# RWKV steps on one core: VectorE adds the old state, and residuals and outputs share one product with it

## The chip, the core and the metric

One core of a Trainium2 chip runs the whole program once: two network blocks on 512 tokens of 1024 channels, in fp32. The metric is the time of the program on the device in microseconds. Times of the rows below come from one profiled execution, counted from the start of its span.

The engines that matter here: TensorE (PE in the rows; PEld is its weight load) multiplies out of SBUF into PSUM banks; VectorE (DVE), ScalarE (ACT) and GpSimd (POOL) work on tiles; SyncE (SP) issues DMAs. Each engine takes its instructions in a fixed order, and semaphores hold an instruction until what it reads or overwrites is ready.

## The reference, cut to what matters

Only the RWKV-7 layer of the second block is touched. For each of 16 heads a state of 64 x 64 is carried through 512 tokens:

```python
def step(state, inp):
    r_t, w_t, k_t, v_t, a_t, b_t = inp
    sa = jnp.einsum('bhij,bhj->bhi', state, a_t)
    state = (state * w_t[:, :, None, :] + sa[..., None] * b_t[:, :, None, :]
             + v_t[..., None] * k_t[:, :, None, :])
    y_t = jnp.einsum('bhij,bhj->bhi', state, r_t)
    return state, y_t
...
_, ys = lax.scan(step, state0, seq_inputs)
```

Around it stand projections, a group norm of the outputs, a bonus term and a gate.

## The kernel before

A scheduler orders each engine's instructions at build time from a simulated timeline; TensorE and the others then run in that order.

The recurrence is computed in blocks of 64 tokens. A chunk is 128 channels, two heads side by side, and its state is a tile `SB` of 128 x 128 whose two 64 x 64 diagonal blocks are the heads' states. A unit is four chunks and half of the tokens, four steps of 64 tokens. Units 0 and 1 are the two halves of the channels in the first 256 tokens, units 2 and 3 the same in the second.

Before a unit's steps, `rwkv_prep` makes the decayed tiles `kr` (the keys' side k and the receptance r), `BN`, `PC` (the decay over a step) and the masked products `G`; `rwkv_inverse1` solves the triangular systems by 31 steps of two operations, each reading the one before (lines L1619 and L1621), on VectorE for units 0, 1 and 3 and on GpSimd for unit 2; ScalarE then copies the result (L1623), and `rwkv_inverse2` finishes on TensorE. After a unit's steps `rwkv_post` normalises the outputs on VectorE and transposes them. The program order is inverse 0, preparation, inverse 1, steps 0, half of the second tokens' preparation, steps 1, inverse 2, post 0, the other half, steps 2, inverse 3, post 1, steps 3, post 2, post 3.

`rwkv_steps` is the part that the change rewrites. `S0` is the old state, `S2` the new. For each of the four steps it goes four times over the four chunks:

- residuals: k against `S0`, plus `G` against the step's values; ScalarE copies them into `R` (L1688)
- corrections: `G` against `R`; ScalarE copies them into `UV` beside the values (L1692)
- new state: the identity against `S0`, plus `BN` against `UV`, added up in PSUM; ScalarE scales by `PC` into `S2` (L1703)
- outputs: r against `S0`, plus `G` against `UV` over all 128 rows; after every second step VectorE copies 128 x 128 outputs of two steps (L1710)

All products are recorded on one line, the helper's L1665. Two PSUM banks hold the four chunks, two chunks each, and the helper keeps the products of one bank in program order. A product in a bank waits for the read of the bank that stands before it in program order.

Of the kernel before, what the change touches and what calls it, by code (L numbers as in the profile page):

```python
# [105 lines left out]
def rwkv_consts():  # L106
    c = Cols()
    c.add("scan", np.tile((np.arange(256) % 64 != 0).astype(np.float32)[None, :], (128, 1)))
    s = np.arange(128)[:, None] % 64
    t = np.arange(64)[None, :]  # L110
    c.add("g", np.concatenate([(s < t), (s <= t)], 1).astype(np.float32))
    c.add("sel", (np.arange(80)[None, :] == 14 + np.arange(128)[:, None] // 64).astype(np.float32))
    return c.array()
# [83 lines left out]
class Core:  # L197
# [1122 lines left out]
    def rwkv(self, x, hn, xsrc):  # L1320

        nc = self.nc
        cst = self.t([128, 464], "cst2", 1)
        nc.gpsimd.dma_start(cst, self.I["cst2"])
        K = self.rk = {}
        K["scan"], K["gmask"] = cst[:, 0:256], cst[:, 256:384]
        sel = lambda m: cst[:, 398 - 2 * m:462 - 2 * m]
        for nm, src, a, b in (("w0h", "w0", 0.5, 0.0), ("a0h", "a0", 0.5, 0.0), ("nkk", "kk", -1.0, 0.0),
# [4 lines left out]
        o = self.voff["mu0"][0]  # L1333
# [5 lines left out]
        K["tmp"] = self.t([128, 256], "itmp", 1)  # L1339
        iv = K["iv"] = self.t([128, 256], "iv", 1)  # L1340

# [5 lines left out]
        K["SB"] = [[self.t([128, 128], "SB", 16) for _ in range(2)] for _ in range(8)]  # L1347
        for a, _ in K["SB"]:
            nc.gpsimd.memset(a, 0.0)

# [13 lines left out]
        def raw(name):  # L1364
# [3 lines left out]

        K["kr"] = [[self.rp.tile([128, 2, 256], F32, tag="rk", bufs=16, name="kr") for _ in range(8)]
                   for _ in range(2)]  # L1370

        def evac(m, i, ps):
            for h in range(2):
                nc.scalar.activation(K["kr"][h][m][:, i, :], ps[:, h * 256:h * 256 + 256], AF.Copy)


        mk, mr, mv = [], [], []
# [133 lines left out]
    def W2(self, name, u):  # L1511
# [6 lines left out]
        return hi, lo  # L1518

    def rwkv_prep(self, c, h, after):  # L1520

# [12 lines left out]
        kr = K["kr"][h][c]  # L1534
        k, r = kr[:, 0, :], kr[:, 1, :]
        r0, r1 = slice(0, 64), slice(64, 128)
# [18 lines left out]
        for g in range(2):  # L1555
            nc.sync.dma_start(nk[64 * g:64 * g + 64], K["ivd"][h, 2 * c + g:2 * c + g + 1].to_broadcast([64, 256]))
        nc.vector.scalar_tensor_tensor(nk, k, cc("nkk"), nk, op0=OP.mult, op1=OP.mult)
        bks = [BK[:, p::2, 1 - p, :] for p in range(2)]
# [4 lines left out]
        nc.vector.tensor_scalar(ta, ta, cc("ka1"), cc("ka2"), op0=OP.mult, op1=OP.add)  # L1563
        nc.vector.tensor_mul(ta, ta, k)
        nc.vector.tensor_mul(k, nk, tw)
        for p in range(2):
            nc.vector.tensor_mul(BK[:, p::2, p, :], ch(ta)[:, p::2], ch(L)[:, p::2])
        nc.vector.scalar_tensor_tensor(nk, r, self.v("rk", c), ta, op0=OP.mult, op1=OP.mult)
        nc.gpsimd.tensor_mul(r, r, Pm)
        return dict(c=c, kr=kr, BK=BK, bk=bk, BN=BN, G=G, PC=PC, rka=nk,  # L1570
                    M=gg.rearrange("q (u x c) -> q u x c", u=4, x=2))

    def rwkv_chunks(self, s):

        nc, K = self.nc, self.rk
        mm = nc.tensor.matmul
        BK, G, kr = s["BK"], s["G"], s["kr"]
        flat = lambda ap: ap.rearrange("p a b -> p (a b)")
        for g in range(2):
            rr = slice(64 * g, 64 * g + 64)  # L1580
            ps = self.bank("sc" if g else "tr")
            for n in range(4):
                mm(ps[:, n * 128:n * 128 + 128], flat(BK[rr, n]), kr[rr, :, n * 64:n * 64 + 64],
                   start=True, stop=True)
            p3, mk = ps.rearrange("p (n s) -> p n s", n=4), K["gmask"].unsqueeze(1).to_broadcast([128, 4, 128])
            nc.vector.tensor_mul(G[:, g], p3, mk)
        tp = self.bank("tr")
        for t in range(2):
            mm(tp[:, 2 * t:2 * t + 2], s["rka"][:, t * 128:t * 128 + 128], self.hsel, start=True, stop=True)
        bon = s["bon"] = self.t([128, 2, 2], "bon", 12)  # L1590
        nc.scalar.activation(bon, tp[:, 0:4].rearrange("p (t h) -> p t h", t=2), AF.Copy)
        for n in range(4):
            nc.tensor.transpose(tp[:, n * 128:n * 128 + 128], flat(BK[:, n]), self.ident)
        nc.scalar.activation(s["bk"], tp, AF.Copy)

    def rwkv_inverse1(self, u, e):
# [8 lines left out]
        for u0, m, o in us:  # L1605
            eng.dma_start(md[o].rearrange("u s t -> s u t"), m[u0:u0 + 64, :, 0:64])
        q0 = u % 2 * 64
# [21 lines left out]
        for b in (1, 0):  # L1629
            for u0, m, o in us:  # L1630
                eng.dma_start(m[u0 + 32 * b:u0 + 32 * b + 32, :, 32 * b:32 * b + 32],
                              md[o, rows(b), rows(b)].rearrange("u s t -> s u t"))
        return ins

    def rwkv_inverse2(self, u, sts):

        nc, K = self.nc, self.rk
        mm = nc.tensor.matmul
        ps = self.bank("av")
        Z = self.t([128, 512], "ea", 4, name="Z").rearrange("p (u s) -> p u s", u=16)  # L1640
        p4 = ps.rearrange("p (u s) -> p u s", u=16)
        G = K["ws"][u][1].rearrange("q (u x c) -> q u x c", u=16, x=2)
        hf = [(slice(64 * (1 - p), 64 * (1 - p) + 32), slice(64 * (1 - p) + 32, 64 * (1 - p) + 64)) for p in range(2)]
        for i in range(16):
            for p, (lo_, hi_) in enumerate(hf):
                mm(p4[hi_, i], G[lo_, i, p, 32:64], K["A11", u % 2][lo_, i], start=True, stop=True)
        for lo_, hi_ in hf:
            nc.scalar.activation(Z[hi_], p4[hi_], AF.Copy)
        for i in range(16):
            for p, (lo_, hi_) in enumerate(hf):  # L1650
                mm(p4[lo_, i], Z[hi_, i], G[hi_, i, p, 32:64], start=True, stop=True)
        for p, (lo_, hi_) in enumerate(hf):
            nc.vector.tensor_copy(G[lo_, :, p, 32:64], p4[lo_])

    def rwkv_steps(self, u, sts):
# [14 lines left out]
        for n in range(4):  # L1670
# [188 lines left out]
```

## Time and profile before

| | us |
|---|---|
| median of 3 runs | 3906.36 (3902.74 to 3907.86) |
| the profiled execution | 3908.79 |
| its span | 3907.0 |
| TensorE busy in the span | 3738.4 (96%) |
| VectorE busy | 1753.8 (45%) |
| ScalarE busy | 1507.1 (39%) |
| GpSimd busy | 1642.4 (42%) |

The span is what the rows count in; the execution's time holds some 2 us around it. The RWKV stage with its recurrence lies around 3030 to 3350 us of the span, where the granted clock of TensorE is lower than elsewhere (0.956 of full speed over the whole span).

### The profile page before, as it was taken

Reading aid. Unit: us, or ns where it says so; the run is one execution under the profiler, and the core shown is the slowest. Engines: PE = TensorE matmul, PEld = TensorE weight load, DVE = VectorE, ACT = ScalarE, POOL = GpSimd, SP = SyncE. Lnnn points to the kernel's source line nnn. Section 1 sums busy time; section 2 is a strip of 40 time slices with the busy share of each in tenths; the row PEclk is TensorE's granted clock in tenths of the full one; section 3 lists DMA queues with packets and bytes.
Section 4 is the critical chain, followed back from the end, with each engine's and each line's share of the span. In section 5 each row is a group of like instructions: output and inputs, shape, how many; then the busy total and the mean of one; then the engine's idle time right before and its main releaser. Section 6 shows DMA issues by size and latency. Waiting matters only on the chain.

```text
span 3907.0 us, 48377 instructions
## 1 busy us (share of the span) xinstructions
PE 3738.4 (96%) x18540; PEld 3000.4 (77%) x18540; DVE 1753.8 (45%) x3587; ACT 1507.1 (39%) x2677; POOL 1642.4 (42%) x900
## 2 busy tenths in 40 slices
PE   9999999999999999999998899999899899799998
PEld 8766777888896677778886777888676777688887
DVE  4553254533545424544436655222568545534123
ACT  4433333433344333334334634332454433343322
POOL 4422436444453233444444563444534321543444
PEclk9999999999999999999998999999999557899999
DMA  5311214233342122232221332222222311321222
GB/s 190 116 54 49 89 60 135 87 97 97 120 152 81 55 67 71 87 114 97 97 95 62 99 106 76 86 93 95 99 85 88 73 41 42 124 102 63 96 97 87
DMA packets 148952, 354.10 MB, mean 91 GB/s; under 512 B 50080, under 2 KB 60864, under 8 KB 148464
## 3 DMA queue, kind: packets, MB, share of 16 engines
q1 hardware_dynamic: 148448, 350.18, 27.6%
q8 instruction: 146, 2.39, 0.3%
q0 software_dynamic: 272, 0.82, 0.1%
q14 instruction: 86, 0.70, 0.1%
HBM read 332.56 MB, written 18.38 MB: 90 GB/s over the span
## 4 chain that ended last, share of the span: by engine, by line
PE 76%; DVE 9%; DMA 5%; POOL 4%; ACT 3%; issue 3%; SPq 0%; POOLq 0%; DVEq 0%; ACTq 0%
PE mm L322 13%; PE mm L323 13%; PE mm L324 13%; PE mm L384 5%; PE mm L383 5%; PE mm L385 5%; PE mm L1665 4%; POOL wlo L285 2%; PE av L383 2%; PE av L385 2%; PE av L384 2%; PE sc L823 2%; PE av L652 1%; PE tr L843 1%; ACT whi L284 1%
## 5 line engine op out<-in xcount | busy, mean ns | idle before, releaser
L285 POOL TENSOR_TENSOR wlo<-wst,whi 128x1024 fp32r<-128x1024 f32 (+2 forms) x524 | 1260.2, 2408 | 1784.2 <-PE mm L324 900.9
L284 ACT ACTIVATE whi<-wst 128x1024 fp32r<-128x1024 f32 (+2 forms) x524 | 548.7, 1048 | 1100.0 <-DMA wst<-in_wu 153.1
L322 PE MATMUL mm<-xTh,whi 128*128 128x512 f32 (+1 forms) x2208 | 833.1, 379 | 13.1 <-ACT whi L284 10.1
L323 PE MATMUL mm<-xTl,whi 128*128 128x512 f32 (+1 forms) x2208 | 835.8, 379 | 0.6
L324 PE MATMUL mm<-xTh,wlo 128*128 128x512 f32 (+1 forms) x2208 | 833.2, 378 | 0.0
L322 PEld LDWEIGHTS mm<-xTh,whi 128*128 128x128 f32 x2208 | 416.6, 190 | 99.8 <-ACT whi L284 11.5
L324 PEld LDWEIGHTS mm<-xTh,wlo 128*128 128x128 f32 x2208 | 418.4, 190 | 84.0 <-issue 8.5
L323 PEld LDWEIGHTS mm<-xTl,whi 128*128 128x128 f32 x2208 | 418.5, 190 | 81.8 <-issue 6.8
L867 DVE SCALAR_TENSOR_TENSOR fup<-mm,vec,fup 128x510 f32<-128x510 f32 (+1 forms) x176 | 131.0, 747 | 220.1 <-ACT fup L865 217.1
L829 ACT ACTIVATE P<-sc,sm 128x128 f32<-128x128 f32 x192 | 100.7, 525 | 203.6 <-DVE sm L827 203.4
L826 DVE TENSOR_TENSOR sc<-sc,cst 128x128 f32<-128x128 f32 x192 | 56.3, 297 | 271.1 <-PE sc L825 256.4
L1160 DVE TENSOR_TENSOR relu<-relu,mm 128x512 f32<-128x512 f32 x64 | 43.8, 687 | 297.6 <-ACT relu L1159 297.6
L384 PE MATMUL mm<-wlo,ph 128*128 128x512 f32 x396 | 156.6, 395 | 0.0
L385 PE MATMUL mm<-whi,pl 128*128 128x512 f32 x396 | 154.6, 395 | 0.0
L383 PE MATMUL mm<-whi,ph 128*128 128x512 f32 x396 | 154.4, 396 | 0.0
L384 PE MATMUL mm<-wlo,xTh 128*128 128x512 f32 (+1 forms) x360 | 137.4, 382 | 5.2 <-POOL wlo L285 5.2
L385 PE MATMUL mm<-whi,xTl 128*128 128x512 f32 (+1 forms) x360 | 136.4, 380 | 0.0
L383 PE MATMUL mm<-whi,xTh 128*128 128x512 f32 (+1 forms) x360 | 132.8, 382 | 3.6 <-ACT whi L284 3.6
L1180 DVE TENSOR_TENSOR work<-work,mm 128x512 f32<-128x512 f32 x60 | 41.2, 687 | 168.1 <-PE mm L385 160.2
L968 PE MATMUL tr<-dg,work 128*128 128x128 f32 x384 | 61.9, 328 | 46.9 <-DVE rsq L416 16.0
L297 POOL TENSOR_TENSOR wres<-wst,wres 128x512 fp32r<-128x512 f32 (+1 forms) x56 | 83.7, 1512 | 37.1 <-ACT wres L296 32.2
L968 PEld LDWEIGHTS tr<-dg,work 128*128 128x128 f32 x384 | 58.8, 240 | 50.3 <-issue 33.6
(580 smaller groups left out, 7431.4 us busy)
## 6 DMA issues: line engine op xcount, KB each, us to landing
wst<-in_wu SPq DMA_DIRECT2D x88, 512.0 KB, 3.6
wst<-in_wmu SPq DMA_DIRECT2D x64, 512.0 KB, 3.6
wst<-in_wmd SPq DMA_DIRECT2D x64, 512.0 KB, 3.6
wst<-in_wg SPq DMA_DIRECT2D x48, 512.0 KB, 3.6
wst<-in_wn SPq DMA_DIRECT2D x44, 512.0 KB, 3.6
wst<-in_wa SPq DMA_DIRECT2D x24, 512.0 KB, 3.6
wst<-in_wb SPq DMA_DIRECT2D x24, 512.0 KB, 3.6
wst<-in_wd SPq DMA_DIRECT2D x24, 512.0 KB, 3.6
```

Source lines behind the costliest of these rows:

```text
L284: nc.scalar.activation(hi, st, AF.Copy)
L285: nc.gpsimd.tensor_sub(lo, st, hi.bitcast(F32))
L322: mm(out, lh, rh, start=start, stop=False)
L323: mm(out, lh, rl, start=False, stop=False)
L324: return mm(out, ll, rh, start=False, stop=stop)
L383: mm(o, xh, hi[:, s], start=k == 0, stop=False)
L384: mm(o, xh, lo[:, s], start=False, stop=False)
L385: mm(o, xl, hi[:, s], start=False, stop=k == nk - 1)
L829: nc.scalar.activation(P[:, o:o + n], sc[:, :n], AF.Exp, bias=mx[:, i:i + 1], accum_out=rs[:, i:i + 1])
L867: nc.vector.scalar_tensor_tensor(a[:, d:], ps[:, :512 - d], self.v(f"fc{l}{tap}", o + j), a[:, d:], op0=OP.mult, op1=OP.add)
L968: nc.tensor.matmul(ps[:, k * 128:k * 128 + 128], work[b][:, k * 128:k * 128 + 128], dg, start=True, stop=True)
L1665: ins = nc.tensor.matmul(*a, **kw, skip_group_check=True)
```

## The change

Three things change in `rwkv_steps`.

The identity product is gone. ScalarE scales the old state into `S2` from SBUF ahead of time (not in a unit's first step from zero, nor in the last), the products of `BN` against `UV` fill a 64-wide part of PSUM, and VectorE writes `S2` = product x `PC` + `S2`, one 64 x 64 operation for each head.

Residuals and outputs share the product with the state: `kr` is laid out step by step, r and k side by side (in the order that puts k on the rows of the residuals), so that one product of 128 columns gives both, and the `G` product of 128 columns adds the values' part of both. One ScalarE copy takes all 128 rows to `R`.

The outputs then need only `G` against the corrections, 64 rows, and VectorE adds the half of `R` to them in every step, in place of a copy after every second one.

In the preparation the mask `gmask` is 256 wide, the views of `kr` are strided, and one VectorE operation becomes two halves; 16 instead of 8 state tiles are cleared on GpSimd, `R` has 8 buffers instead of 7, and the small tile `iv` moves into a shared pool.

```diff
-        for a, _ in K["SB"]:
-            nc.gpsimd.memset(a, 0.0)
+        for ab in K["SB"]:
+            for a in ab:
+                nc.gpsimd.memset(a, 0.0)
...
-        nc.vector.scalar_tensor_tensor(nk, r, self.v("rk", c), ta, op0=OP.mult, op1=OP.mult)
-        nc.gpsimd.tensor_mul(r, r, Pm)
+        for a in range(2):
+            nc.vector.scalar_tensor_tensor(lr(nk)[:, a], r[:, a], self.v("rk", c), lr(ta)[:, a], op0=OP.mult, op1=OP.mult)
+        nc.gpsimd.tensor_mul(r, r, lr(Pm))
...
-            S0 = [K["SB"][c0 + i][1 - p] for i in range(4)]
-
-            Yp, Rp = ([banks[i // 2][:, (2 * (i % 2) + j) * 128:(2 * (i % 2) + j) * 128 + 128] for i in range(4)]
-                      for j in range(2))
+            S0, S2 = ([K["SB"][c0 + i][a] for i in range(4)] for a in (1 - p, p))
+
+
+            A, B = ([banks[i // 2][:, (2 * (i % 2) + j) * 128:(2 * (i % 2) + j) * 128 + 128] for i in range(4)]
+                    for j in range(2))
             R = []
             for i, s in enumerate(sts):
                 if not first:
-                    mm(i, Rp[i][ur], s["kr"][:, 0, ns], S0[i], start=True, stop=False)
+                    mm(i, A[i], s["kr"][:, n * 128:n * 128 + 128], S0[i], start=True, stop=False)
                 for g, hs in enumerate(hs2):
-                    mm(i, Rp[i][ur, hs], s["G"][vr, g, n, 0:64], UV[vr, i, hs], start=first, stop=True)
-                R.append(self.t([128, 128], "R", 7))
-                nc.scalar.activation(R[i][ur], Rp[i][ur], AF.Copy)
+                    mm(i, A[i][:, hs], s["G"][vr, g, n, :], UV[vr, i, hs], start=first, stop=True)
+                R.append(self.t([128, 128], "R", 8))
+                nc.scalar.activation(R[i], A[i], AF.Copy)
+            if not first and not last:
+                for i, s in enumerate(sts):
+                    nc.scalar.activation(S2[i], S0[i], AF.Copy, scale=s["PC"][:, n:n + 1])
             for i, s in enumerate(sts):
                 for g, hs in enumerate(hs2):
-                    mm(i, Rp[i][ur, hs], s["G"][ur, g, n, 0:64], R[i][ur, hs], start=True, stop=True)
-                nc.scalar.activation(UV[ur, i], Rp[i][ur], AF.Copy)
+                    mm(i, B[i][ur, hs], s["G"][ur, g, n, ur], R[i][ur, hs], start=True, stop=True)
+                nc.scalar.activation(UV[ur, i], B[i][ur], AF.Copy)
             for i, s in enumerate(sts if not last else ()):
-                S2 = K["SB"][c0 + i][p]
-                if first:
-                    mm(i, Rp[i], s["BN"][:, n], UV[:, i], start=True, stop=True)
-                    for hs in hs2:
-                        nc.scalar.activation(S2[hs, hs], Rp[i][hs, hs], AF.Copy, scale=s["PC"][hs, n:n + 1])
-                    continue
-                mm(i, Rp[i], self.ident, S0[i], start=True, stop=False)
                 for hs in hs2:
-                    mm(i, Rp[i][hs, hs], s["BN"][:, n, hs], UV[:, i, hs], start=False, stop=True)
-                nc.scalar.activation(S2, Rp[i], AF.Copy, scale=s["PC"][:, n:n + 1])
+                    mm(i, B[i][hs, 0:64], s["BN"][:, n, hs], UV[:, i, hs], start=True, stop=True)
+                for hs in hs2:
+                    if first:
+                        nc.scalar.activation(S2[i][hs, hs], B[i][hs, 0:64], AF.Copy, scale=s["PC"][hs, n:n + 1])
+                    else:
+                        nc.vector.scalar_tensor_tensor(S2[i][hs, hs], B[i][hs, 0:64], s["PC"][hs, n:n + 1],
+                                                       S2[i][hs, hs], op0=OP.mult, op1=OP.add)
             for i, s in enumerate(sts):
-                if not first:
-                    mm(i, Yp[i][vr], s["kr"][:, 1, ns], S0[i], start=True, stop=False)
                 for g, hs in enumerate(hs2):
-                    mm(i, Yp[i][vr, hs], s["G"][:, g, n, 64:128], UV[:, i, hs], start=first, stop=True)
-                if p:
-                    nc.vector.tensor_copy(s["BN"][:, n // 2, :], Yp[i])
+                    mm(i, A[i][vr, hs], s["G"][ur, g, n, vr], UV[ur, i, hs], start=True, stop=True)
+                nc.vector.tensor_add(s["BN"][vr, n // 2, :], A[i][vr], R[i][vr])
```

How the scheduler then orders the engines is shown at three places. In these rows `ws`, `wse` and `hn` are pieces of large buffers that hold `G`, `BN` and `UV`, `mm` is a PSUM bank of the steps, `kr`, `SB`, `R`, `PC` are as above and `cst` is the identity; `x2` is two instructions that read alike. The first is TensorE in unit 3's steps, before:

```order
L1665 MATMUL mm<-ws,wse 64x64 x2
L1665 MATMUL mm<-SB,cst 128x128
L1665 MATMUL mm<-ws,wse 64x64 x2
L1665 MATMUL mm<-SB,kr 64x128
L1665 MATMUL mm<-ws 64x64 x2
L1665 MATMUL mm<-SB,kr 64x128
L1665 MATMUL mm<-ws 64x64 x2
L1665 MATMUL mm<-SB,kr 64x128
L1665 MATMUL mm<-ws 64x64 x2
L1665 MATMUL mm<-SB,cst 128x128
L1665 MATMUL mm<-ws,wse 64x64 x2
```

and after (the product line is now L1682):

```order
L1682 MATMUL mm<-SB,kr 128x128
L1682 MATMUL mm<-ws 128x64 x2
L1682 MATMUL mm<-R,ws 64x64 x4
L1682 MATMUL mm<-ws,wse 64x64 x2
L1682 MATMUL mm<-R,ws 64x64 x2
L1682 MATMUL mm<-ws,wse 64x64 x4
L1682 MATMUL mm<-ws 64x64 x2
L1682 MATMUL mm<-ws,wse 64x64 x2
L1682 MATMUL mm<-ws 64x64 x4
L1682 MATMUL mm<-SB,kr 128x128
L1682 MATMUL mm<-ws 128x64 x2
```

The rows SB,cst are gone, and of the state's products with kr one of 128 x 128 stands where two of 64 x 128 stood.

The second is VectorE in the inverse of unit 3 while unit 2's steps run. M, A and itmp are the inverse's tiles, and L1728 is the first reduction of unit 1's normalisation. Before:

```order
L1621 TENSOR_TENSOR A<-A,itmp 64x6x26
L1619 TENSOR_TENSOR itmp<-M,A 64x135
L1710 COPY ws<-mm 128x128
L1621 TENSOR_TENSOR A<-A,itmp 64x5x27
L1728 TENSOR_REDUCE sm_25522<-ws 128x4
L1619 TENSOR_TENSOR itmp<-M,A 64x112
L1710 COPY ws<-mm 128x128
L1621 TENSOR_TENSOR A<-A,itmp 64x4x28
L1710 COPY ws<-mm 128x128
L1728 TENSOR_REDUCE sm_25522<-ws 128x4
L1619 TENSOR_TENSOR itmp<-M,A 64x87
```

and after, a little later in the inverse (its lines are now L1636 and L1638):

```order
L1721 SCALAR_TENSOR_TENSOR SB<-mm,PC,SB 64x64 x2
L1638 TENSOR_TENSOR A<-A,itmp 64x4x28
L1767 TENSOR_TENSOR o<-o,tr 128x256
L1636 TENSOR_TENSOR itmp<-M,A 64x87
L1721 SCALAR_TENSOR_TENSOR SB<-mm,PC,SB 64x64 x2
L1768 TENSOR_TENSOR o<-o,tr 128x256
L1638 TENSOR_TENSOR A<-A,itmp 64x3x29
L1721 SCALAR_TENSOR_TENSOR SB<-mm,PC,SB 64x64 x2
L1726 TENSOR_TENSOR ws<-mm,R 64x128
L1636 TENSOR_TENSOR itmp<-M,A 64x60
L1638 TENSOR_TENSOR A<-A,itmp 64x2x30
L1721 SCALAR_TENSOR_TENSOR SB<-mm,PC,SB 64x64 x2
```

Where a copy of outputs stood now and then, the state additions L1721 and the output adds L1726 (of unit 2, at first also of unit 1) stand among the inverse's operations; 28 of the former and 12 of the latter stand between the inverse's first and last row, and 8 copies stood there before.

The third is VectorE in the normalisation of unit 0 (L395 to L401 and L1740, now L1756), beside unit 1's steps. Before:

```order
L399 TENSOR_TENSOR rsw<-rsw 128x16
L400 TENSOR_TENSOR rsw<-rsw 128x16
L401 SCALAR_TENSOR_TENSOR rsw<-rsw 128x16
L1740 TENSOR_TENSOR wse<-wse,rsw 128x256 x4
L1751 TENSOR_TENSOR o<-o,tr 128x256
L1752 TENSOR_TENSOR o<-o,tr 128x256
L1710 COPY wse<-mm 128x128 x2
L1751 TENSOR_TENSOR o<-o,tr 128x256
```

and after:

```order
L399 TENSOR_TENSOR rsw<-rsw 128x16
L400 TENSOR_TENSOR rsw<-rsw 128x16
L401 SCALAR_TENSOR_TENSOR rsw<-rsw 128x16
L1756 TENSOR_TENSOR wse<-wse,rsw 128x256 x4
L1767 TENSOR_TENSOR o<-o,tr 128x256
L1726 TENSOR_TENSOR wse<-mm,R 64x128
L1768 TENSOR_TENSOR o<-o,tr 128x256
L1726 TENSOR_TENSOR wse<-mm,R 64x128
L1767 TENSOR_TENSOR o<-o,tr 128x256
L1721 SCALAR_TENSOR_TENSOR SB<-mm,PC,SB 64x64 x2
```

Output adds of unit 1 stand behind fifteen rows of this normalisation (of which the last are shown), as two copies of outputs did before, and unit 1's state additions stand behind them.

## Rows read from the trace of the kernel before

**Rows 1.** Stretches: us; busy us (count) of PE, PEld, DVE, ACT, POOL; PEclk; DMA.

```profile
3040.00:3073.00 33.00, 29.14 (x194) 25.50 (x194) 31.19 (x85) 13.24 (x37) 5.25 (x8) 0.50 0.21 68
3070.00:3115.00 45.00, 43.14 (x406) 34.08 (x405) 17.11 (x45) 14.80 (x43) 22.29 (x41) 0.65 0.28 57
3115.00:3225.00 110.00, 108.28 (x669) 84.73 (x670) 46.31 (x122) 39.19 (x111) 28.89 (x52) 0.50 0.17 39
3225.00:3271.00 46.00, 43.49 (x346) 33.73 (x347) 39.73 (x114) 18.74 (x61) 7.61 (x12) 0.80 0.07 21
3285.00:3330.00 45.00, 42.56 (x337) 33.42 (x336) 5.90 (x17) 15.08 (x48) 10.01 (x12) 0.81 0.17 56
```

**Rows 2.** Chain that ended last, in order of time, around the end of C.

```profile
3270.96 2.12 ACT M L1623
```

**Rows 3.** Line L1665, 3070 to 3115: passes; idle us, times until L1688.

```profile
L1665 PE MATMUL mm<-SB,kr x40: 272/421/476, 3071.1 to 3111.4; 128*64 128x128 f32 x40
...
L1665 PE MATMUL mm<-SB,cst x20: 275/422/582, 3084.8 to 3114.8; 128*128 128x128 f32 x20
...
  ACT R L1688: 1.9, 4
```

**Rows 4.** Line L1665, 3115 to 3225: passes; idle us, times until L1688.

```profile
L1665 PE MATMUL mm<-SB,kr x64: 421/421/476, 3117.3 to 3222.7; 128*64 128x128 f32 x64
...
L1665 PE MATMUL mm<-SB,cst x31: 421/422/583, 3114.8 to 3224.5; 128*128 128x128 f32 x31
...
  ACT R L1688: 1.0, 2
```

**Rows 5.** Line L1665, 3225 to 3271: passes; durations in ns.

```profile
L1665 PE MATMUL mm<-SB,kr x64: 272/323/473, 3225.1 to 3266.8; 128*64 128x128 f32 x64
...
L1665 PE MATMUL mm<-SB,cst x22: 271/377/582, 3226.3 to 3255.3; 128*128 128x128 f32 x22
```

**Rows 6.** Line L1665, 3271 to 3330: passes; idle us, times until L1688.

```profile
L1665 PE MATMUL mm<-SB,kr x56: 272/275/421, 3294.1 to 3328.8; 128*64 128x128 f32 x56
...
L1665 PE MATMUL mm<-SB,cst x24: 275/418/582, 3288.5 to 3317.2; 128*128 128x128 f32 x24
...
  ACT R L1688: 5.2, 12
```

**Rows 7.** Timeline of TensorE in E: start us, us, operation.

```profile
3303.22 0.80 PE L1665 MATMUL mm<-SB,cst 128*128 128x128 f32 x2
3303.95 0.48 PE L1665 MATMUL mm<-ws,wse 128*64 128x64 f32 x4
3304.22 0.63 PE L1665 MATMUL mm<-SB,kr 128*64 128x128 f32 x2
3304.65 0.63 PE L1665 MATMUL mm<-ws 128*64 128x64 f32 x4
```

**Rows 8.** The same timeline, some ten us later.

```profile
3314.80 0.49 PE L1665 MATMUL mm<-SB,cst 128*128 128x128 f32 x2
...
3315.22 0.34 PE L1665 MATMUL mm<-ws,wse 128*64 128x64 f32 x4
...
3315.39 0.39 PE L1665 MATMUL mm<-SB,kr 128*64 128x128 f32 x2
...
3315.61 0.39 PE L1665 MATMUL mm<-ws 128*64 128x64 f32 x4
```

**Rows 9.** VectorE's groups by form, 3040 to 3330: busy us, mean ns, idle before.

```profile
L1619 DVE TENSOR_TENSOR itmp<-M,A 64x60 f32<-64x60 f32 x4 | 0.9, 218 | 0.1
...
L401 DVE SCALAR_TENSOR_TENSOR rsw<-rsw 128x16 f32<-128x16 f32 x9 | 1.9, 213 | 0.3
```

**Rows 10.** The same view for VectorE in C, 3225 to 3271.

```profile
L1710 DVE COPY ws<-mm 128x128 f32<-128x128 f32 x8 | 2.3, 291 | 1.5 <-PE mm L1665 1.4
```

**Rows 11.** VectorE's waits in C: us in total, times, longest.

```profile
DVE ws L1710 <- PE mm L1665: 1.4, 4, 0.6
```

**Rows 12.** GpSimd's groups, 2800 to 2824: busy us, mean ns.

```profile
L1349 POOL MEMSET SB<- 128x128 f32 x8 | 1.2, 223 | 0.0
```

More of the change, by code (lines that the diff above doesn't have):

```diff
@@ L110, in rwkv_consts @@
     t = np.arange(64)[None, :]
-    c.add("g", np.concatenate([(s < t), (s <= t)], 1).astype(np.float32))
+    c.add("g", np.concatenate([(s <= t), (s < t), (s < t), (s <= t)], 1).astype(np.float32))
     c.add("sel", (np.arange(80)[None, :] == 14 + np.arange(128)[:, None] // 64).astype(np.float32))
@@ L1322, in rwkv @@
         nc = self.nc
-        cst = self.t([128, 464], "cst2", 1)
+        cst = self.t([128, 592], "cst2", 1)
         nc.gpsimd.dma_start(cst, self.I["cst2"])
         K = self.rk = {}
-        K["scan"], K["gmask"] = cst[:, 0:256], cst[:, 256:384]
-        sel = lambda m: cst[:, 398 - 2 * m:462 - 2 * m]
+        K["scan"], K["gmask"] = cst[:, 0:256], cst[:, 256:512]
+        sel = lambda m: cst[:, 526 - 2 * m:590 - 2 * m]
         for nm, src, a, b in (("w0h", "w0", 0.5, 0.0), ("a0h", "a0", 0.5, 0.0), ("nkk", "kk", -1.0, 0.0),
@@ L1339, in rwkv @@
         K["tmp"] = self.t([128, 256], "itmp", 1)
-        iv = K["iv"] = self.t([128, 256], "iv", 1)
+        iv = self.t([128, 256], "eb", 4, name="iv")
         b = [self.big([128, KC, S], F32R, f"mx{i}") for i in range(3)]
@@ L1367, in raw @@
             return w
-        K["kr"] = [[self.rp.tile([128, 2, 256], F32, tag="rk", bufs=16, name="kr") for _ in range(8)]
+        K["kr"] = [[self.rp.tile([128, 512], F32, tag="rk", bufs=16, name="kr") for _ in range(8)]
                    for _ in range(2)]
@@ L1373, in evac @@
             for h in range(2):
-                nc.scalar.activation(K["kr"][h][m][:, i, :], ps[:, h * 256:h * 256 + 256], AF.Copy)
+                to = self.kr_views(K["kr"][h][m])[i]
+                src = ps[:, h * 256:h * 256 + 256]
+                nc.scalar.activation(to, self.like(src, i), AF.Copy)
         mk, mr, mv = [], [], []
@@ L1518, in W2, with kr_views, like @@
         return hi, lo
+    def kr_views(self, a):
+        return (a.rearrange("p (a w) -> p a w", a=2)[:, :, 64:192],
+                a.rearrange("p (a b s) -> p a b s", a=2, b=4)[:, :, 0::3, :])
+    def like(self, ap, i):
+        if i == 0:
+            return ap.rearrange("p (a w) -> p a w", a=2)
+        return ap.rearrange("p (a b s) -> p a b s", a=2, b=2)
     def rwkv_prep(self, c, h, after):
@@ L1534, in rwkv_prep @@
         kr = K["kr"][h][c]
-        k, r = kr[:, 0, :], kr[:, 1, :]
+        k, r = self.kr_views(kr)
+        lk, lr = (lambda ap: self.like(ap, 0)), (lambda ap: self.like(ap, 1))
         r0, r1 = slice(0, 64), slice(64, 128)
@@ L1556, in rwkv_prep @@
             nc.sync.dma_start(nk[64 * g:64 * g + 64], K["ivd"][h, 2 * c + g:2 * c + g + 1].to_broadcast([64, 256]))
-        nc.vector.scalar_tensor_tensor(nk, k, cc("nkk"), nk, op0=OP.mult, op1=OP.mult)
+        nc.vector.scalar_tensor_tensor(lk(nk), k, cc("nkk"), lk(nk), op0=OP.mult, op1=OP.mult)
         bks = [BK[:, p::2, 1 - p, :] for p in range(2)]
@@ L1563, in rwkv_prep @@
         nc.vector.tensor_scalar(ta, ta, cc("ka1"), cc("ka2"), op0=OP.mult, op1=OP.add)
-        nc.vector.tensor_mul(ta, ta, k)
-        nc.vector.tensor_mul(k, nk, tw)
+        nc.vector.tensor_mul(lk(ta), lk(ta), k)
+        nc.vector.tensor_mul(k, lk(nk), lk(tw))
         for p in range(2):
             nc.vector.tensor_mul(BK[:, p::2, p, :], ch(ta)[:, p::2], ch(L)[:, p::2])
-        nc.vector.scalar_tensor_tensor(nk, r, self.v("rk", c), ta, op0=OP.mult, op1=OP.mult)
-        nc.gpsimd.tensor_mul(r, r, Pm)
+        for a in range(2):
+            nc.vector.scalar_tensor_tensor(lr(nk)[:, a], r[:, a], self.v("rk", c), lr(ta)[:, a], op0=OP.mult, op1=OP.mult)
+        nc.gpsimd.tensor_mul(r, r, lr(Pm))
         return dict(c=c, kr=kr, BK=BK, bk=bk, BN=BN, G=G, PC=PC, rka=nk,
@@ L1582, in rwkv_chunks @@
             for n in range(4):
-                mm(ps[:, n * 128:n * 128 + 128], flat(BK[rr, n]), kr[rr, :, n * 64:n * 64 + 64],
+                mm(ps[:, n * 128:n * 128 + 128], flat(BK[rr, n]), kr[rr, n * 128:n * 128 + 128],
                    start=True, stop=True)
-            p3, mk = ps.rearrange("p (n s) -> p n s", n=4), K["gmask"].unsqueeze(1).to_broadcast([128, 4, 128])
-            nc.vector.tensor_mul(G[:, g], p3, mk)
+            p3, mk = ps.rearrange("p (n s) -> p n s", n=2), K["gmask"].unsqueeze(1).to_broadcast([128, 2, 256])
+            nc.vector.tensor_mul(G[:, g].rearrange("p (n m) s -> p n (m s)", m=2), p3, mk)
         tp = self.bank("tr")
@@ L1605, in rwkv_inverse1 @@
         for u0, m, o in us:
-            eng.dma_start(md[o].rearrange("u s t -> s u t"), m[u0:u0 + 64, :, 0:64])
+            eng.dma_start(md[o].rearrange("u s t -> s u t"), m[u0:u0 + 64, :, u0:u0 + 64])
         q0 = u % 2 * 64
@@ L1630, in rwkv_inverse1 @@
             for u0, m, o in us:
-                eng.dma_start(m[u0 + 32 * b:u0 + 32 * b + 32, :, 32 * b:32 * b + 32],
+                eng.dma_start(m[u0 + 32 * b:u0 + 32 * b + 32, :, u0 + 32 * b:u0 + 32 * b + 32],
                               md[o, rows(b), rows(b)].rearrange("u s t -> s u t"))
@@ L1645, in rwkv_inverse2 @@
             for p, (lo_, hi_) in enumerate(hf):
-                mm(p4[hi_, i], G[lo_, i, p, 32:64], K["A11", u % 2][lo_, i], start=True, stop=True)
+                mm(p4[hi_, i], G[lo_, i, p, hi_], K["A11", u % 2][lo_, i], start=True, stop=True)
         for lo_, hi_ in hf:
@@ L1650, in rwkv_inverse2 @@
             for p, (lo_, hi_) in enumerate(hf):
-                mm(p4[lo_, i], Z[hi_, i], G[hi_, i, p, 32:64], start=True, stop=True)
+                mm(p4[lo_, i], Z[hi_, i], G[hi_, i, p, hi_], start=True, stop=True)
         for p, (lo_, hi_) in enumerate(hf):
-            nc.vector.tensor_copy(G[lo_, :, p, 32:64], p4[lo_])
+            nc.vector.tensor_copy(G[lo_, :, p, hi_], p4[lo_])
     def rwkv_steps(self, u, sts):
```

## Prediction

> **What bounds the kernel now.** I read the stretches of the recurrence first, because only they change: the table of busy times cuts the RWKV stage into the pieces that follow one another [rows 1]. The reader should see four different regimes. Up to about 3073 us VectorE is the bound (31.19 of 33 us busy). Stretch A, 3070 to 3115, holds the steps of unit 0; TensorE is busy 43.14 of 45 us at a granted clock of 0.65. In stretch B, 3115 to 3225 (unit 1's steps, the second half's preparation, the start of unit 2), TensorE is busy 108.28 of 110 us at 0.50, which is 1.2 GHz: here a product removed is time removed, unless a wait takes its place. In C, 3225 to 3271, unit 2's steps run beside the serial inverse of unit 3 on VectorE; TensorE has 43.49 and VectorE 39.73 of 46 us, and C ends when ScalarE can read the finished inverse at 3270.96 [rows 2]. In E, 3285 to 3330, only unit 3's steps and pieces of unit 1's output are left: TensorE 42.56 of 45 us at 0.81, VectorE 5.90.
>
> Then I read the step's matmul line for each stretch: how many products of each kind lie in it, and what TensorE waited for [rows 3 to 6]. Each product is recorded as two passes. The identity products (tiles SB and cst) number 10, 15.5, 11 and 12 in A, B, C and E; products of the state with kr number 20, 32, 32 and 28, half of them for residuals and half for outputs. The waits for ScalarE's residual copy tell how often a hand-off from TensorE to a reading engine and back is seen as a hole in TensorE: 4 times for 10 residuals in A (0.48 us each), 2 for 16 in B (0.50), 12 for 14 in E (0.43). In B the other bank's products and the preparation cover it; in E nothing does.
>
> **What is removed.** The price of a product is the distance of starts on TensorE, not its recorded duration, since products overlap. At the low clock the identity pair takes 3303.22 to 3303.95 = 0.73 us and the kr pair 3304.22 to 3304.65 = 0.43 us [rows 7]; at 2.4 GHz they take 0.42 and 0.22 us [rows 8]. All identity products go, and the kr product of the outputs goes since one product of 128 columns now serves both (the pass streams the same 128 columns of the state, so I price the merged one like one of the old ones; a dearer one would be at most the 0.42 of the 128 x 128 identity pair, plus 0.2 us for each of the 56).
>
> Granted clocks of 0.65 and 0.80 mean 70% and 40% of the time at the low level, so an identity pair costs 0.64 and 0.54 us there, and a kr pair 0.37 and 0.30. Removed from TensorE:
> A: 10 x 0.64 + 10 x 0.37 = 10.1 us. B: 15.5 x 0.73 + 16 x 0.43 = 18.2. E: 12 x 0.54 + 14 x 0.30 = 10.7. C: 10.7 as well, but VectorE's inverse sets C's end, so I count nothing for it.
>
> **What is added.** ScalarE's read of a new state is replaced by two VectorE operations of 64 x 64; that hand-off existed before. No row shows this operation: the nearest are a scalar_tensor_tensor of 128 x 16 at 0.21 us and a tensor_tensor of 64 x 60 at 0.22 [rows 9], so 0.23, between 0.21 and 0.29 (the 128 x 128 copy out of PSUM, which is larger) [rows 10]. The output's add of 64 x 128 I price like that copy, 0.29; before it was a copy after every second step only, after it is an add in each step, and the next product in that bank waits for it. So the new waits are those of the outputs, one for each, and I let each be seen as often as the residual's hand-off is seen now in the same stretch.
>
> A: 10 x 4/10 x 0.48 = 1.9 given back, -8.2 net.
> B: 16 x 2/16 x 0.50 = 1.0; VectorE is busy 46.31 of 110 us with operations of 46.31/122 = 0.38 us, so a read finds it busy with a chance of 0.42 and waits half an operation, 0.08 us; 31.5 reads give 2.5. In the new order some of unit 1's output adds stand behind fifteen operations of unit 0's normalisation, 15 x 0.38 = 5.7 us; TensorE has the second half's preparation to do meanwhile, and I charge a quarter, 1.5. Net -13.2.
> E: 14 x 12/14 x 0.43 = 5.2 given back, -5.5 net.
>
> C gets longer. The new order puts 28 state additions and 12 output adds among the inverse's 62 operations, and takes 8 copies out: 28 x 0.23 + 12 x 0.29 - 8 x 0.29 = 7.6 us of VectorE. VectorE runs in order, so the inverse also waits whenever an addition waits for its product. Today's 8 copies there wait 1.4 us together [rows 11], 0.18 each; 40 additions give 7.0. VectorE now has 46 - 39.73 = 6.3 us free. +7.6 + 7.0 - 6.3 = +8.3.
>
> Two small ones: four output adds of unit 0's first step fall into the VectorE-bound start, 4 x 0.29 = +1.2. Eight more memsets of 0.22 us each on GpSimd [rows 12] are 1.8 us at the start of the stage; nothing if GpSimd is ahead, all if the normalisation there waits, so +0.9. ScalarE's 48 scalings of the old state read SBUF and lie in its idle time (18.74 of 46 us busy in C), and the DMAs keep their number and queues: nothing.
>
> Sum: -8.2 - 13.2 + 8.3 - 5.5 + 1.2 + 0.9 = -16.5 us. The profiled execution took 3908.79, which is 2.4 above the median 3906.36 of the runs. 3908.8 - 16.5 - 2.4 = 3890 us.
>
> **Bounds.** Let e be the share of hand-offs to VectorE that are seen. With e = 0: -10.1 - 18.2 + 1.3 - 10.7 = -37.7, and with the small terms of B's queue and the start about -31.6. With e = 1, states included: 20 x 0.48 in A, 31.5 x 0.50 in B, 40 x 0.43 in C, 26 x 0.43 in E, together 53.8. So the sum is -31.6 + 53.8 e; my forecast is e = 0.28. It is zero at 0.59, and it leaves the band of 0.2% (8 us, about what a measurement of this kernel tells from no change) at 0.44 and at 0.73.
>
> **The rule against it.** The Trainium skill, Perfetto Trace Analysis, "Optimizing Tensor Performance", says that independent groups of matmuls should rotate through different PSUM banks, so that the read-out of one overlaps the products of the next. By that rule, with four states in two banks and each bank held in program order, every hand-off is exposed and the sum would be that of e = 1. The trace agrees in E (12 of 14 seen) and not in B (2 of 16), so it speaks for a middle value.
>
> **Rivals.**
> First, slower: VectorE's queue becomes the step's pace. The place is C and, by the same mechanism, each bank turn elsewhere: an addition waits behind an operation of the inverse, TensorE waits for the addition, and the next product's addition finds the next inverse operation ahead of it. For it speaks that VectorE is 86% busy in C and 42% in B. Against it: the 8 copies that stand there now wait 0.18 us on average, and VectorE is nearly idle in E. It decides from e = 0.73 on; at 0.85 the sum is +14.1, 3920 us.
> Second, nothing to see: waits of ScalarE give way to waits of VectorE and eat what the products free, e about 0.6, 3906 us. For it: in E the residual's waits are exposed nearly always, and a bank has eight hand-offs in a step where six or seven were.
> Third, the clock. The granted clock swings between 1.2 and 2.4 GHz inside C and E. If fewer and more scattered products leave E at the low level throughout, then of its 42.56 us of products 62% ran at full clock; about 20 us of them are left after the change, and they would take some 1.8 times as long (0.73 to 0.42, 0.43 to 0.22), 16 us, of which the 5.2 us of waits cover a part: +11, sum -5.5, 3901 us. Against it: B, with the fewest holes, has the lower clock now.
> The Trainium skill, TensorE: Matmul & The Clock Gate, "A second HAM failure mode: psum-queue depth-cycling", describes a kernel whose small idle times between groups in cycling banks made the clock swing and cost throughput. The swing is in this trace too (0.50 in B, 0.80 in C); that more holes lower it is not, as B shows.
> Fourth, all of it is kept: the two banks cover each other and the additions slip into the inverse's gaps, e near 0, with the first terms alone -35 to -37: 3869 to 3873 us. For it speaks B, a third of the stage's time, with 98% busy.
>
> **Chances.** The forecast 0.49 (its own range 3877 to 3902, e from 0.05 to 0.5); slower by the queue 0.18; nothing to see 0.15; the clock 0.08; all kept 0.10. Faster by over 0.2%: 0.46 of the first and the last, 0.56. Within: 0.03 + 0.15 + 0.08 = 0.26. Slower: 0.18. The range leaves out half of the case "all kept" and the dearer half of the slow case: 3868 to 3918.
>
> **What would show it.** In the trace after: no SB,cst products, kr products at half their count, and TensorE's busy time on the step's line lower by 40 to 50 us; B shorter by about 13 us and still over 95% busy; C longer, VectorE over 90% busy in it; E shorter by about 5 us, with TensorE's idle time put down to VectorE's lines instead of ScalarE's. I am wrong in size if B's busy share drops below 90% (e was higher there), wrong in kind if C is longer by over 15 us, and wrong about the merged product if the kr pair's distance of starts is well above 0.43 and 0.22 us.

## The result and the profile after

The changed kernel takes 3926.1 us (3923.7 to 3931.81, 4 runs) beside 3905.26 for the kernel before: ratio 1.0055, interval 1.0038 to 1.0073. It is slower by 20.8 us, where 16 us less were forecast. The profiled execution took 3925.38 us, its span is 3923.6, the mean granted clock 0.946 (before 0.956).

The stretches of the recurrence, cut by the preparation and the inverse as in [rows 1] (A, B, C and E), in the table of busy times of the changed kernel, columns as there:

```profile
3071.00:3112.00 41.00, 37.79 (x304) 30.74 (x303) 20.62 (x61) 10.94 (x29) 19.89 (x38) 0.50 0.29 59
3112.00:3220.00 108.00, 104.51 (x630) 85.06 (x630) 56.64 (x170) 41.89 (x121) 29.78 (x52) 0.50 0.16 37
3220.00:3267.00 47.00, 43.28 (x235) 34.30 (x235) 38.96 (x123) 15.34 (x46) 7.43 (x12) 0.50 0.07 21
...
3283.00:3348.00 65.00, 63.42 (x377) 49.72 (x373) 25.44 (x85) 18.08 (x55) 11.69 (x14) 0.65 0.13 44
```

A went from 45 to 41 us, B from 110 to 108, C from 46 to 47, the piece between C and E from 14 to 16, E from 45 to 65. That is +17, the whole difference of the spans (16.6). The steps do not keep to these cuts, though: by the passes of `G` against `R` on TensorE, the corrections of 13, 19, 12, 1.5 and 14.5 chunks lay in the five pieces (four passes each), and now 8, 21, 11, 4 and 16. So A's 4 us less are no gain. E takes 20 us more for 1.5 chunks more, and 19 products of a projection (lines L383 to L385) have moved into it: they stood at 3267.8 to 3274.0 and stand at 3289.7 to 3297.7 now, 7.4 us of TensorE.

Two things should be seen. TensorE is 97% busy in B and 98% in E, with fewer products on the step's line. And the granted clock is 0.50 through A, B and C, where it was 0.65, 0.50 and 0.80; in E it is 0.65, was 0.81.

The step's matmul line is busy longer, though it holds 1098 records in place of 1296. First the kernel before, then the changed one, both from 3028 to 3366 us, columns: length, TensorE busy, weight loads busy, clock, DMA:

```profile
3028.00:3366.00 338.00, 181.87 (x1296) 138.62 (x1296) 0.64 0.23 59
```
```profile
3028.00:3366.00 338.00, 200.33 (x1098) 156.45 (x1097) 0.56 0.20 50
```

The timeline of TensorE in unit 3's steps of the changed kernel, at the low clock (start, recorded duration):

```profile
3313.36 1.44 PE L1682 MATMUL mm<-ws 64*64 64x64 f32 x8
3314.73 0.79 PE L1682 MATMUL mm<-SB,kr 128*128 128x128 f32 x2
...
3317.11 0.79 PE L1682 MATMUL mm<-SB,kr 128*128 128x128 f32 x2
3317.83 1.11 PE L1682 MATMUL mm<-ws 64*128 64x64 f32 x4
3318.87 0.79 PE L1682 MATMUL mm<-SB,kr 128*128 128x128 f32 x2
```

And the kernel before at the same clock, a residual's turn and, further down, an output's:

```profile
3125.99 0.63 PE L1665 MATMUL mm<-SB,kr 128*64 128x128 f32 x2
3126.56 0.69 PE L1665 MATMUL mm<-ws,hn 64*64 64x64 f32 x4
3127.18 0.69 PE L1665 MATMUL mm<-SB,kr 128*64 128x128 f32 x2
...
3306.21 0.64 PE L1665 MATMUL mm<-SB,kr 128*64 128x128 f32 x2
3306.64 0.63 PE L1665 MATMUL mm<-ws 128*64 128x64 f32 x4
3307.07 0.63 PE L1665 MATMUL mm<-SB,kr 128*64 128x128 f32 x2
```

From start to start, the shared product with the state takes 0.72 us where the residual's took 0.57 (0.56 to 0.62 over this trace), and the G product behind it 1.04 where it took 0.62. Both now load 128 columns (128\*128, 64\*128) in place of 64. So the residual's turn costs 1.76 us in place of 1.19. The outputs' turn falls from 0.43 + 0.43 to 0.68 only (8 passes in 1.37), since its G product, now on 64 rows, takes 0.25 more than it did on 128. The shared product and its G products together are therefore 0.57 - 0.18 = 0.39 us dearer than the two turns they replace; what is saved is the identity pair's 0.73 [rows 7]. A chunk's step saves 0.73 + 0.18 - 0.57 = 0.34 us at the low clock; the forecast had 0.73 + 0.43 = 1.16.

Loaded columns are not the whole price. The outputs' G product loads 64 columns before and after, and the narrow kr product took 0.43 us before a G product of 128 rows and 0.57 before one of 64 rows. No run isolates what the 64 rows cost.

The Trainium skill, TensorE: Matmul & The Clock Gate, "LDWEIGHTS (loading the stationary operand)", says that the load's time goes with the loaded columns and not with the rows. The trace agrees in the order, not in the size: in the two kernels' stretches at the low clock the recorded loads of 128 x 128 (kr after, cst before) and of 64 x 128 have a mean of 0.31 to 0.32 us, those of 128 x 64 and 64 x 64 of 0.21 to 0.23, where the formula there gives 0.11 and 0.05. The rule says which products would get dearer; the prediction did not use it.

VectorE's additions took about what they were given: the state's 0.283 us where 0.23 was forecast, the outputs' 0.287, as priced (the state's group by form, changed kernel, 3028 to 3350; count, busy us, mean ns, idle before):

```profile
L1721 DVE SCALAR_TENSOR_TENSOR SB<-mm,PC,SB 64x64 f32<-64x64 f32 x96 | 27.2, 283 | 53.8 <-PE mm L1682 49.1 <-ACT ws L1713 3.0
```

The idle time is VectorE waiting for TensorE, not the other way round. What TensorE waited for on the step's line (us, times), before and after:

```profile
  ACT R L1688: 12.7, 29
...
  ACT SB L1703: 4.8, 9
```
```profile
  DVE SB L1721: 16.2, 35
  ACT ws L1713: 9.0, 19
  DVE wse L1726: 5.4, 11
...
  ACT R L1706: 0.9, 2
```

### The profile page after: what moved, and what is told of

The parts are those of the page before. It is cut to its first block, busy times and chain, and to the rows that moved or that the text cites. A ratio compares the mean times of both kernels' runs of the same rounds, so it can differ in the third digit from the quotient of the medians.

```text
span 3923.6 us, 48159 instructions
## 1 busy us (share of the span) xinstructions
PE 3758.9 (96%) x18348; PEld 3023.1 (77%) x18348; DVE 1782.4 (45%) x3731; ACT 1507.0 (38%) x2677; POOL 1646.8 (42%) x908
## 4 chain that ended last, share of the span: by engine, by line
PE 77%; DVE 9%; DMA 4%; POOL 4%; ACT 3%; issue 2%; SPq 0%; POOLq 0%; DVEq 0%; ACTq 0%
PE mm L322 13%; PE mm L324 13%; PE mm L323 13%; PE mm L384 5%; PE mm L383 5%; PE mm L385 5%; PE mm L1682 4%; POOL wlo L285 2%; PE av L383 2%; PE av L385 2%; PE av L384 2%; PE sc L823 2%; PE av L652 1%; PE tr L843 1%; PE tr L968 1%
## 5 line engine op out<-in xcount | busy, mean ns | idle before, releaser
L385 PE MATMUL mm<-whi,pl 128*128 128x512 f32 x396 | 154.7, 396 | 0.0
L383 PE MATMUL mm<-whi,ph 128*128 128x512 f32 x396 | 154.5, 396 | 0.0
L385 PE MATMUL mm<-whi,xTl 128*128 128x512 f32 (+1 forms) x360 | 138.3, 386 | 0.0
L383 PE MATMUL mm<-whi,xTh 128*128 128x512 f32 (+1 forms) x360 | 133.8, 385 | 3.7 <-ACT whi L284 3.7
```

Source lines behind the costliest of these rows:

```text
L383: mm(o, xh, hi[:, s], start=k == 0, stop=False)
L385: mm(o, xl, hi[:, s], start=False, stop=k == nk - 1)
```

## The experiments

Ten kernels in three sessions, each session on another chip and beside the kernel before on that chip. The medians of before were 3910.49 (e1 to e4), 3913.43 (e5 to e8) and 3911.49 us (e9, e10), its median clock 0.954 to 0.955. The ratio to the kernel before is the one on record, with its 95% interval, and compares runs of one session; it is not the quotient of the two medians (for e2 and e4 these give 1.0109 and 1.0130). 0.001 of it is 4 us. The clock below is the median over a kernel's runs. The scheduler orders each of these kernels anew, so an edit of one line can move other instructions too; no run holds the order fixed.

| kernel | median us | ratio to before | clock |
|---|---|---|---|
| the full change | 3926.1 | 1.0055 (1.0038 to 1.0073) | 0.946 |
| e1 state only | 3891.21 | 0.9960 (0.9942 to 0.9979) | 0.959 |
| e2 share only | 3953.23 | 1.0125 (1.0107 to 1.0143) | 0.9435 |
| e3 narrow G | 3913.1 | 1.0012 (1.0000 to 1.0024) | 0.948 |
| e4 idle identity | 3961.17 | 1.0143 (1.0128 to 1.0158) | 0.9425 |
| e5 copy each step | 3908.4 | 0.9979 (0.9967 to 0.9990) | 0.954 |
| e6 wide kr | 3925.12 | 1.0029 (1.0018 to 1.0040) | 0.9485 |
| e7 no old state | 3901.38 | 0.9959 (0.9941 to 0.9978) | 0.953 |
| e8 wide G | 3939.55 | 1.0070 (1.0057 to 1.0083) | 0.947 |
| e9 narrow identity | 3883.89 | 0.9935 (0.9917 to 0.9953) | 0.960 |
| e10 idle identity on e1 | 3906.95 | 0.9989 (0.9976 to 1.0003) | 0.958 |

**The two halves, each alone: e1 and e2.** e1 is the kernel before with the state's part (residuals and outputs keep their products):

```diff
+            if not first and not last:
+                for i, s in enumerate(sts):
+                    nc.scalar.activation(S2[i], S0[i], AF.Copy, scale=s["PC"][:, n:n + 1])
...
-                mm(i, Rp[i], self.ident, S0[i], start=True, stop=False)
...
+                    mm(i, Rp[i][hs, 0:64], s["BN"][:, n, hs], UV[:, i, hs], start=True, stop=True)
...
+                        nc.vector.scalar_tensor_tensor(S2[i][hs, hs], Rp[i][hs, 0:64], s["PC"][hs, n:n + 1],
+                                                       S2[i][hs, hs], op0=OP.mult, op1=OP.add)
```

> The kernel before with the first half of the change alone: VectorE adds the scaled old state to the product, and residuals and outputs keep their own narrow products. Theory W (the price on TensorE goes with the columns of the loaded operand, so the shared 128-column products give back what the identity products free): here nothing gets wider, 48 identity pairs of 0.73 or 0.42 us go, 20 to 35 us of TensorE; about 3885 to 3895 us. Theory H (VectorE's hand-offs set the pace): the state is handed over through VectorE as in the full change, so no faster than before, 3905 to 3925. Theory C (the granted clock is what costs the time): C and E stay at the low level as in the full change, and the time comes out near 3905.

e2 is the full change with the identity product, the BN products behind it and ScalarE's scaled read put back (the lines marked - for the new state in the diff of the change):

> The full change without its first half: residuals and outputs share the 128-column products and VectorE adds the outputs in every step, while the identity product and ScalarE's scaled read make the new state as before. W: a chunk's step costs TensorE at the low clock 0.72 + 1.04 + 0.61 where it cost 0.43 + 0.61 + 0.43 + 0.43, so 0.47 us more for each of 56: slower than before by 15 to 26 us, 3920 to 3930. H: only the 64 output adds are new, slower than before by 5 to 10, 3910 to 3915. C: the identity products are there again, so the clock is as before and the time at most 3910.

Measured: e1 is faster than before, 0.9960, as W said. e2 is far slower, 1.0125, 43 to 49 us, nearly twice the most that W expected of it (26). The state's half is good, the sharing is what costs. H and C are wrong on both; with the identity products there, e2's clock is lower still.

**Narrow and wide G: e3 and e8.** e3 edits the full change:

```diff
-                    mm(i, A[i][:, hs], s["G"][vr, g, n, :], UV[vr, i, hs], start=first, stop=True)
+                    mm(i, A[i][ur, hs], s["G"][vr, g, n, ur], UV[vr, i, hs], start=first, stop=True)
...
-                    mm(i, A[i][vr, hs], s["G"][ur, g, n, vr], UV[ur, i, hs], start=True, stop=True)
+                    mm(i, A[i][vr, hs], s["G"][:, g, n, vr], UV[:, i, hs], start=True, stop=True)
...
```

(in a unit's first step from zero VectorE then copies the outputs, since there is nothing to add).

> The full change with one edit: the product of G with the values fills the 64 residual columns only, and the outputs' G product runs over all 128 rows again as before; the shared product with the state and both VectorE additions stay. W: 1.04 + 0.61 becomes 0.61 + 0.43 at the low clock, 0.6 us less for each of 64 chunk steps: 20 to 35 us faster than the full change, 3892 to 3906. H: the hand-offs are those of the full change, 3920 to 3928. C: TensorE has still less work and the clock stays low, 3915 to 3926.

Measured: 1.0012 beside the full change's 1.0055, some 17 us of the 21 back (13 by the medians), at about the same clock (0.948 and 0.946). W expected 20 to 35 back, H at most 6, C at most 11: it lies between them, nearest to W.

**The identity as idle work: e4.**

```diff
+                if not first:
+                    mm(i, B[i], self.ident, S0[i], start=True, stop=True)
```

> The full change with the identity product put back as idle work: it is written into the bank ahead of the state's products, which then overwrite it, and nobody reads it. W: 48 pairs of 0.73 us more on a TensorE that is the bound, 15 to 35 us slower than the full change, 3940 to 3960. H: TensorE waits for VectorE anyway, so about the full change's 3926, up to 3932. C: if the wide identity product is what brought the full clock in C and E, they return to it, and the time falls to 3905 to 3920.

Measured: 1.0143, 35 us over the full change, the upper end of what W said and 48 times the pair's 0.73; TensorE is the bound of the changed kernel. The clock does not come back.

**Hand-offs and widths apart: e5, e6, e8, e7.** e5 takes the widths back and leaves the hand-offs:

```diff
-                    mm(i, A[i], s["kr"][:, n * 128:n * 128 + 128], S0[i], start=True, stop=False)
+                    mm(i, A[i][ur], s["kr"][:, n * 128 + 64 * (1 - p):n * 128 + 64 * (1 - p) + 64], S0[i], start=True, stop=False)
...
+                if not first:
+                    mm(i, A[i][vr], s["kr"][:, n * 128 + 64 * p:n * 128 + 64 * p + 64], S0[i], start=True, stop=False)
...
-                nc.vector.tensor_add(s["BN"][vr, n // 2, :], A[i][vr], R[i][vr])
+                nc.vector.tensor_copy(s["BN"][vr, n // 2, :], A[i][vr])
```

(and e3's two edits of G). 

> The full change with narrow products throughout: residuals and outputs have their own 64-column products with the state as before, VectorE adds the old state, and VectorE copies the outputs in every step (64 x 128) where e1 copied every second step. So it is e1 with the output hand-offs of the full change. W (TensorE's price goes with the columns of the loaded operand): TensorE's work is e1's, 10 to 18 us under the kernel before, granted clock as in e1. H (VectorE's hand-offs): 64 reads in place of 32, the gain of e1 is mostly gone, 5 us under to 5 us over the kernel before, and the low clock of the full change comes with the holes.

e6 is e5 with the first of these lines as in the full change:

> The previous kernel with one edit: the residual's product with the state loads all 128 columns of kr and writes 128 rows, of which the outputs' half is not used and is overwritten later. W at one clock: 0.71 us in place of 0.51 for each of 56 pairs, 8 to 11 us slower than the previous kernel. C2 (wide products also bring the low granted clock): 15 to 30 us slower, with the low clock through C and E. H: nothing, within 4 us.

e8 is e5 with the wide G product of the full change:

> e5 with one edit: the product of G with the values loads 128 columns (its outputs' half is not used and is overwritten later). W at one clock: 1.02 us in place of 0.58 for each of 64 chunk steps, 15 to 25 us slower than e5. C2: the same and the low clock through C and E, 25 to 40 us slower. H: nothing, within 4 us of e5.

e7 leaves the old state's share out of the new state:

```diff
-                    nc.scalar.activation(S2[i], S0[i], AF.Copy, scale=s["PC"][:, n:n + 1])
...
-                        nc.vector.scalar_tensor_tensor(S2[i][hs, hs], Rp[i][hs, 0:64], s["PC"][hs, n:n + 1],
-                                                       S2[i][hs, hs], op0=OP.mult, op1=OP.add)
+                    nc.scalar.activation(S2[i][hs, hs], Rp[i][hs, 0:64], AF.Copy, scale=s["PC"][hs, n:n + 1])
```

> e1 with the old state's share of the new state left out of the computation: no scaling ahead and no VectorE addition, ScalarE writes the two 64 x 64 blocks of product times decay as in a first step. TensorE's work is that of e1. W: VectorE's additions cost TensorE nothing, so within 4 us of e1, about 16 under the kernel before. H: the state's hand-off through VectorE and its in-order queue cost 8 to 15 us, so 24 to 32 under the kernel before.

Measured: e7 equals e1 (0.9959 and 0.9960, each with some 7 us on either side), so VectorE's addition of the state and ScalarE's scaling cost nothing that shows. e5 lies 0.0019 over e1, some 7 us for 64 output hand-offs in place of 32 (with the new layout of kr), between W and H; the two intervals overlap, so these 7 us are not clear of noise. From e5 to e6 the ratio rises by 0.0050 (20 us; 17 by the medians), to e8 by 0.0091 (36 us; 31 by the medians), and the clock falls from 0.954 to 0.9485 and 0.947. That is C2's sum, not W's at one clock. The table of busy times from 3030 to 3340 shows it, e5, e6 and then the full change:

```profile
3030.00:3340.00 310.00, 270.34 (x2139) 213.77 (x2139) 196.72 (x576) 119.29 (x335) 90.88 (x139) 0.64 0.22 54
```
```profile
3030.00:3340.00 310.00, 277.19 (x2048) 224.74 (x2049) 184.62 (x536) 111.09 (x320) 77.34 (x131) 0.54 0.20 48
```
```profile
3030.00:3340.00 310.00, 290.69 (x1932) 235.60 (x1933) 179.38 (x535) 108.13 (x312) 76.68 (x130) 0.53 0.19 46
```

**Narrow identity: e9, and the identity on e1: e10.** e9 is the kernel before, without any of the change:

```diff
-                mm(i, Rp[i], self.ident, S0[i], start=True, stop=False)
...
+                    mm(i, Rp[i][hs, hs], self.ident[:, hs], S0[i][:, hs], start=True, stop=False)
...
-                nc.scalar.activation(S2, Rp[i], AF.Copy, scale=s["PC"][:, n:n + 1])
+                for hs in hs2:
+                    nc.scalar.activation(S2[hs, hs], Rp[i][hs, hs], AF.Copy, scale=s["PC"][hs, n:n + 1])
```

> The kernel before with one edit and nothing of the change: the identity product of 128 x 128 is split into its two diagonal blocks of 64 loaded columns, and ScalarE reads the new state as two blocks of 64 x 64. W (wide loads are dear): the two narrow products cost about what the pair with BN costs, 0.41 in place of 0.70 us at the low clock for each of 48, minus 0.25 us more of ScalarE in the hand-off: 5 to 15 us under the kernel before. C2 (wide loads bring the low clock): the clock rises above 0.956 as well and the time falls by 15 to 25. If neither holds: within 5 us of the kernel before.

e10 puts e4's two lines into e1:

> e1 (VectorE adds the old state, narrow products) with the identity product put back as idle work that the state's products overwrite. W at one clock: 48 pairs of 0.70 or 0.41 us, 20 to 30 us slower than e1, so 4 to 14 us over the kernel before, at e1's granted clock of 0.959. C2: the clock falls as well, to 0.950 or below, and the time is 20 or more over the kernel before. H (TensorE waits for VectorE in e1 anyway): within 8 us of e1.

Measured: e9 has the lowest time of all, 0.9935, about 25 us under the kernel before, the upper end of what C2 expected; against e1 the intervals overlap. The edit also gives ScalarE two small reads in place of one. Its line's rows show the identity with 64 loaded columns:

```profile
L1666 PE MATMUL mm<-SB,cst x192: 222/314/370, 3077.3 to 3299.7; 128*64 128x64 f32 x192
```

e10 lies 0.0029 over e1 by the ratios, 11 us, between H (8 at most) and W (20 to 30), and its clock is e1's (0.958 and 0.959). So not every wide product brings the low clock; C2 is wrong there. The same 48 products cost 35 us in the full change (e4).

**The clock between runs of one program.** Over the 56 runs of the kernel before in the three sessions the mean clock lies between 0.951 and 0.961 and the time between 3898.49 and 3920.5 us; a straight line through them falls by 2.1 us for each 0.001 (correlation -0.91). In the edited kernels with six or more runs it is 1.5 (e3) to 2.8 (e5). The full change has 0.946 beside 0.955: 9 x 2.1 = 19 us, nearly the whole loss. By the same line 12 of the 17 to 20 us from e5 to e6 and 15 of the 31 to 36 from e5 to e8 go with the clock. This is an estimate and not shown by an edit of its own: no run changed the clock and left the work. Nor does the line say which way it goes. A program that is longer in a stretch at 0.50 has a lower mean for that alone, about 0.002 for 20 us.

## Why the prediction was wrong

The step that failed is in "What is removed": "I price the merged one like one of the old ones". It gave a dearer one at most 0.2 us, and it did not count at all that the G product behind it loads 128 columns too. Measured, the merged pair costs 0.15 more, this G 0.42 more, and the outputs' G on 64 rows 0.25 more: of the 1.16 us that a chunk's step frees, 0.82 are given back, and 0.34 are left. The bound of 0.2 was taken at 2.4 GHz; at the low clock [rows 7] had the identity pair of the same 128 x 128 form at 0.73, which is what the merged pair took. e6 and e8 show both widths one at a time, and e3 takes the wide G out of the full change. The removal itself was priced rightly: the identity pair was worth its place (e4), and e1 alone gained 16 us, with TensorE still 96% busy from 3115 to 3215, as said.

The 40 chunk steps that the sum counts in A, B and E make 0.82 x 40 = 33 us at the low clock. With them the sum would be +16 in place of -16.5, an estimate, near the +20.8.

A second error is the weight of the clock rival. It stood at 0.08, for E alone and +11 us. The clock fell in A, C and E, by 0.009 or 0.010 over the program, and by the line between runs that is again the size of the loss. The two accounts overlap and can't be added: the 33 us are priced at the low clock, where part of these steps had run at the high one. The reason given against the rival, that B with the fewest holes had the lower clock, still holds: e5 leaves TensorE idle for 40 of 310 us and has 0.64 there, the full change 19 and 0.53. The Trainium skill, TensorE: Matmul & The Clock Gate, "A second HAM failure mode: psum-queue depth-cycling", has short idle times between groups make the clock swing; these runs don't show that. What in the wide products lowers it stays open: in e6 and e8 it comes with one edit, in e10 it doesn't.

C, +8.3 in the forecast, was +1. The inverse still set its end: ScalarE's copy of it starts at 3267.30, 47 us after B's end, released by VectorE's last step of the inverse at 3267.08. Among the inverse's operations stood 28 state additions of 0.28 us, which waited 4.3 us for TensorE, the output adds 0.2, and not the 7.0 forecast for all:

```profile
L1721 DVE SCALAR_TENSOR_TENSOR SB<-mm,PC,SB 64x64 f32<-64x64 f32 x28 | 7.9, 283 | 4.8 <-PE mm L1682 4.3
```

VectorE's busy time in C even fell, from 39.73 to 38.96, since the normalisation of unit 2, which had begun in C, left it. For unit 2's steps, whose products had ended with C at 3267, now ran on at the low clock: the first reductions of their normalisation start between 3281.8 and 3288.3, before between 3263.1 and 3267.4, and E began with them unfinished. I took the inverse for the end of C and counted TensorE's part for nothing.

The hand-offs (e = 0.28) were near: TensorE's holes on the step's line went from 17.5 to 31.5 us by the releasers shown, +14, and e5 against e1 makes the added output reads worth some 7, within noise. The slow rival came out on the right side by another mechanism: e1 has holes of 17.2 us behind its state additions alone and is faster than before. The rule on rotating PSUM banks that the prediction weighed would have given the sign, and with e = 1 nearly the size (+22), but not for its reason: the holes grew by 14 us, and e = 1 stood for 53.8.

B, forecast at -13.2, gave -2, with the corrections of 21 chunks in place of 19: it stayed bound by TensorE, and TensorE had nearly as much to do. E, forecast at -5.5, gave +20: the dearer products, the lower clock, the rest of unit 2 and the 7.4 us of the projection meet there, and no run tells them apart.

One reading was off and weighs little: of A's 20 products with kr, 12 are residuals and 8 outputs, not ten and ten, so A had 0.7 us less to lose.

## What to carry to other kernels

Price a small fp32 product by its form, loaded rows and columns, and not by how many products there are. Merging two 64-column products with the state into one of 128 saved 0.28 us at the low clock, but it gave the G products forms that cost 0.67 more. Splitting one 128-column identity product into its two useful blocks, the opposite edit, came with 25 us less. Before a term is summed, price also the products that take another form from a merge, from rows of that form at the same clock. And where the granted clock swings in the stretch that changes, look at the clock of each kernel as well as its time: between runs of one program a hundredth of it went with some 20 us, more than any term of the sum.

## What was not expected of the hardware

Between runs of one unchanged program the time went with the mean granted clock, 2.1 us for 0.001, over a range of 22 us. And the low level, 1.2 GHz, held from 3029 to 3294 us in the full change with TensorE 97% busy in B, while the kernels with narrow products, which left TensorE idle more, had the higher clock from 3030 to 3340 us (0.64 in e5, 0.65 in e1 and e9, beside 0.53). A small fp32 product of 64 loaded columns took longer on 64 rows than on 128 (0.68 beside 0.43 us for four passes at the low clock).
